# A two-layer hybrid transformer block on one core: three convolution taps per attention step, attention tiles in a list of their own, norm chunks ahead of context adds, modulation bias per four pairs

## The chip, the core and the metric

The kernel runs on one core of a Trainium2 chip. The metric is the time of one execution in microseconds (us) on the device. A core has five engines that each work through a queue of instructions in order and wait for each other by semaphores: TensorE (PE; PEld is its weight load), VectorE (DVE), ScalarE (ACT), GpSimd (POOL) and SyncE (SP), whose queue here issues the DMAs. TensorE writes into PSUM; everything else lies in SBUF.

## The reference, cut to what matters

Two layers act on 512 latent tokens and 256 context tokens of width 1024, all in fp32. The context goes through the same weights with another modulation, and in layer 1 only its keys and values are needed.

```
mod = silu(c) @ w_mod + b_mod            # shift, scale, gate, twice
xn = rms_norm(x) * (1 + scale1) + shift1
p = xn @ w_in                            # q, k, v | Fourier | conv | pool columns
attn = softmax(rope(norm(q)) @ rope(norm(k)).T) @ v      # 4 query heads, 2 key heads
four = real(fft2(p_f)) @ w_f
conv = silu(layer_norm(depthwise31(a * sigmoid(b)) + bias)) @ w_pw
pool = (window means - u) @ w_pool * scale
x = x + gate1 * (concat(attn, four, conv, pool) @ w_out)
xn = rms_norm(x) * (1 + scale2) + shift2
x = x + gate2 * ((silu(xn @ w_a) * (xn @ w_g)) @ w_ffn_out)   # inner width 2816
```

## The kernel before

Activations lie transposed: a tile has 128 channels on the partitions and tokens along the free axis (512 latent, then 256 context). Every fp32 product is made of three fp32r matmuls (`mm3`, line 315) on operands split into a rounded part and a remainder, so each weight is loaded raw by a DMA, rounded by ScalarE and subtracted by GpSimd or VectorE (`split`, line 180).

SBUF is handed out in lists of buffers. `W` (line 77) has 14 buffers of 1024 columns: raw weights, their two parts, modulation weights, and the transposed probabilities `pt` of attention. `AL` (line 74) has 28 buffers of 768 columns: normalized inputs, mixer outputs, Fourier pieces, and the query tiles `qst` and `qT`. A tile takes a buffer when it is first written, in the order in which the program asks, and gives it back after its last reader. PSUM has two buffers each of three kinds; the kind `PB` (two banks) holds the scores `S`, the running sum `run` of the convolution and the gate products. Within these rules a scheduler orders each engine's queue by a simulated time line, with the order of the program as priority; it looks at what is ready, so an instruction can run well ahead of its place.

Each layer has a mixer (`mix_phase`, line 599) and a feed-forward part (`ffn`, line 1204).

In the mixer, the projection to q, k and v comes first. Then the loop of line 1110 runs over attention tiles (one block of 128 queries and one head; 24 in layer 0, of which the last 8 are context queries with only 256 keys, 16 in layer 1) plus two steps. Step i computes the scores of tile i and their softmax (`soft`: maximum on VectorE, line 995; exp and scale on ScalarE), takes one pair of modulation columns from `mod_pairs` (two 512 KB weight loads, 16 small matmuls, a transpose, a sum, a bias add in line 344), lets `fill` take other projection work (columns for convolution, pooling and Fourier, then the Fourier mixer, then the convolution's layer norm) by declared costs in us at `pace.fill` per step, transposes and multiplies with v the tile of step i - 2 (`flip`), and pulls convolution taps:

```
pull(pace.taps0)
for i in range(len(tiles) + 2):
    ...
    if i >= pace.step0:
        pull(pace.taps)
        for _ in range(pace.side): next(side, None)
pull(99)
```

A tap is one VectorE instruction over all tokens of a block of 128 channels (line 669). The convolution has 31 taps and two blocks; of block 1 the first `side_n` taps (10 in layer 0, 8 in layer 1) run on ScalarE and GpSimd. `taps0`, `step0` and `taps` are 6, 3, 2 in layer 0 and 10, 2, 2 in layer 1. `tail` (line 1078) begins the layer norm after the convolution (`conv_out`) only when the generator of taps is exhausted; until then it gives Fourier work, and then nothing. What is left is written after the loop, behind the taps that are left and the casts of the attention outputs (`mix_at`). The output projection follows: 8 output blocks, of which the last four are held for the second half of the tokens.

In the feed-forward part of layer 0 a chunk of 128 inner channels is done by a seven-product scheme (`fast`, line 1251): `load_ff` (line 229) loads the two weight columns of a chunk raw, and makes seven operands of them, each in one `W` buffer. The first two chunks are done directly (`fast_first`, line 1227). After every two chunks `out_step` (line 1355) multiplies with the output weights and adds to x, latents first, then context; in the last step it also squares x for the next norm, whose reciprocal root is made by `n1.rstd`. The normalized chunks (`apply`, line 454) are written in the next layer's mixer. Layer 1's feed-forward part uses plain products (`ag`, line 1343).

## Time and profile before

| | us |
|---|---|
| median of 3 runs | 1476.47 (1474.7 to 1476.76) |
| the profiled execution | 1474.25 |
| its span, first to last instruction | 1472.5 |
| TensorE busy | 1417.3 (96%) |
| VectorE busy | 945.2 (64%) |
| ScalarE busy | 600.2 (41%) |
| GpSimd busy | 199.3 (14%) |

Busy time is what the engine's instructions cover. TensorE's matmuls overlap in the records and their ends are modelled, so a stretch that is all busy need not be at its peak. PEclk is the clock that TensorE was granted, 1.00 being 2.4 GHz and 0.50 being 1.2 GHz. The stages in the profiled execution, roughly: start and first projection to 76 us, the rest of layer 0's mixer to 336 us, its feed-forward part to 874 us, layer 1's mixer to 1102 us, its feed-forward part to the end.

### The profile page before, as it was taken

How to read it: one execution, taken by the hardware profiler on the slowest of the kernel's cores; microseconds unless marked ns; L12 is line 12 of the kernel's file. 1: busy time of each engine (PE TensorE's matmuls, PEld its weight loads, DVE VectorE, ACT ScalarE, POOL GpSimd, SP SyncE). 2: the span in 40 equal slices, each digit the busy share in tenths (PEclk: the TensorE clock that was granted, in tenths of full speed). 3: DMA queues.
4: the chain of work that ended last, by engine and by line, in shares of the span. 5: the costliest groups of instructions: out<-in, count | busy, mean ns of one | idle time of the engine just before them, and what ended most of it. 6: DMA issues, size and time to landing. Idle time of an engine off the chain costs nothing.

```text
span 1472.5 us, 20702 instructions
## 1 busy us (share of the span) xinstructions
PE 1417.3 (96%) x8298; PEld 1217.2 (83%) x8298; DVE 945.2 (64%) x1572; ACT 600.2 (41%) x1035; POOL 199.3 (14%) x161
## 2 busy tenths in 40 slices
PE   7999988999999999999999989999899999999998
PEld 4787766998998999999999968776698888888887
DVE  3569577247986778686877777866545545444444
ACT  4457656436533233332332345666544322222220
POOL 2526420420000000000000035430240000000000
PEclk9999989999999999999999999999999999999999
DMA  9525433320323133222322233356442323333231
GB/s 297 164 87 165 157 110 107 109 71 26 104 70 103 54 91 114 87 68 76 115 86 58 92 111 92 117 169 211 127 114 80 108 86 90 111 101 100 89 98 57
DMA packets 192928, 157.35 MB, mean 107 GB/s; under 512 B 6464, under 2 KB 179520, under 8 KB 192832
## 3 DMA queue, kind: packets, MB, share of 16 engines
q1 hardware_dynamic: 192544, 155.34, 34.4%
q8 instruction: 65, 1.06, 0.3%
q10 hardware_dynamic: 288, 0.69, 0.1%
q14 instruction: 31, 0.25, 0.1%
HBM read 151.81 MB, written 4.19 MB: 106 GB/s over the span
## 4 chain that ended last, share of the span: by engine, by line
PE 83%; DVE 7%; ACT 4%; DMA 4%; issue 1%; POOL 1%; SPq 0%; ACTq 0%; DVEq 0%; POOLq 0%
PE ag L161 35%; PE fo L161 20%; PE wo L161 6%; PE qkv L161 4%; PE cv L161 3%; PE agl L161 3%; PE mod L161 3%; DVE run L669 3%; PE u L161 2%; PE ssq L161 1%; PE S L161 1%; DMA wm<-in_w_mod_dram 1%; PE pv L161 1%; PE PT L167 1%; PE cc L161 1%
## 5 line engine op out<-in xcount | busy, mean ns | idle before, releaser
L1362 DVE SCALAR_TENSOR_TENSOR x<-fo,mod,x 128x512 f32<-128x512 f32 (+1 forms) x264 | 170.7, 657 | 81.0 <-PE fo L161 80.5
L161 PE MATMUL fo<-hl,foh 128*128 128x512 f32 (+1 forms) x528 | 187.7, 356 | 0.0
L161 PE MATMUL fo<-hh,fol 128*128 128x512 f32 (+1 forms) x528 | 187.4, 356 | 0.0
L161 PE MATMUL fo<-hh,foh 128*128 128x512 f32 (+1 forms) x528 | 185.5, 358 | 1.9 <-DVE x L1362 1.4
L161 PE MATMUL ag<-t,fs 128*128 128x384 f32 x720 | 136.6, 336 | 0.9 <-DVE hg L1266 0.9
L161 PEld LDWEIGHTS ag<-t,fs 128*128 128x128 f32 x720 | 125.0, 188 | 6.4 <-issue 1.6
L161 PEld LDWEIGHTS fo<-hh,foh 128*128 128x128 f32 x528 | 99.0, 188 | 16.1 <-DVE x L1362 1.8
L161 PEld LDWEIGHTS fo<-hh,fol 128*128 128x128 f32 x528 | 99.2, 188 | 15.1 <-issue 0.2
L161 PEld LDWEIGHTS fo<-hl,foh 128*128 128x128 f32 x528 | 99.2, 188 | 14.7 <-issue 0.7
L182 ACT CAST foh<-fo 128x1024 fp32r<-128x1024 f32 x44 | 46.2, 1050 | 146.0 <-DMA fo<-in_w_ffn_out_dram 146.0
L161 PE MATMUL ag<-b,fa 128*128 128x384 f32 x480 | 92.6, 336 | 1.5 <-DVE ht L1216 1.5
L105 DVE TENSOR_TENSOR fol<-fo,foh 128x1024 fp32r<-128x1024 f32 x44 | 53.8, 1222 | 54.1 <-ACT foh L182 41.9
L669 DVE SCALAR_TENSOR_TENSOR run<-glu,vt,run 128x512 f32<-128x512 f32 (+1 forms) x98 | 87.0, 887 | 1.0
L161 PEld LDWEIGHTS ag<-b,fa 128*128 128x128 f32 x480 | 83.4, 188 | 3.4 <-DVE ht L1216 1.8
L242 ACT CAST fs<-ff 128x512 fp32r<-128x512 f32 x80 | 45.4, 620 | 75.0 <-DVE ff L246 53.0
L437 POOL TENSOR_TENSOR acca<-acca,sq 128x512 f32<-128x512 f32 (+1 forms) x4 | 4.5, 1117 | 523.8 <-ACT sq L436 523.8
L161 PE MATMUL wo<-mxh,wol 128*128 128x384 f32 (+2 forms) x224 | 73.7, 330 | 0.0
L161 PE MATMUL wo<-mxl,woh 128*128 128x384 f32 (+2 forms) x224 | 73.5, 329 | 0.0
L161 PE MATMUL wo<-mxh,woh 128*128 128x384 f32 (+2 forms) x224 | 73.5, 331 | 0.1
L161 PE MATMUL ag<-xfh,fah 128*128 128x512 f32 (+1 forms) x192 | 71.3, 376 | 1.2 <-ACT xfh L465 1.2
L161 PE MATMUL ag<-xfl,fah 128*128 128x512 f32 (+1 forms) x192 | 71.6, 373 | 0.8 <-DVE xfl L466 0.8
L242 ACT CAST fa<-ff 128x512 fp32r<-128x512 f32 x60 | 35.6, 619 | 90.2 <-PE ag L161 51.7
(319 smaller groups left out, 3308.1 us busy)
## 6 DMA issues: line engine op xcount, KB each, us to landing
wm<-in_w_mod_dram SPq DMA_DIRECT2D x64, 512.0 KB, 4.4
fo<-in_w_ffn_out_dram SPq DMA_DIRECT2D x44, 512.0 KB, 3.3
ff<-in_w_ffn_in_dram SPq DMA_DIRECT2D x40, 512.0 KB, 4.7
fa<-in_w_ffn_in_dram SPq DMA_DIRECT2D x24, 512.0 KB, 4.4
fg<-in_w_ffn_in_dram SPq DMA_DIRECT2D x24, 512.0 KB, 3.9
wm<-in_w_mod_dram SPq DMA_DIRECT2D x40, 256.0 KB, 5.3
wo<-in_w_out_dram SPq DMA_DIRECT2D x16, 512.0 KB, 4.8
wm<-in_w_mod_dram SPq DMA_DIRECT2D x16, 384.0 KB, 3.3
```

The lines of the kernel that those rows point to most:

```text
L105: eng.tensor_tensor(out=out, in0=full, in1=b32(hi), op=ALU.subtract)
L161: i = last_pe[0] = pe.matmul(*a, **kw)
L167: i = last_pe[0] = pe.transpose(*a)
L182: act.copy(out=hi[:, :n], in_=raw[:, :n])
L242: act.copy(out=hi, in_=full)
L437: eng.tensor_tensor(out=a, in0=a, in1=t[:, sl], op=ALU.add)
L669: yield dve.scalar_tensor_tensor(out=cacc[b][:, :cwid] if j == CONVW - 1 else run, in0=glu[b][:, j:j + cwid], scalar=tap(b, j), in1=cacc[b ...
L1362: dve.scalar_tensor_tensor(out=x[m][:, sl], in0=ps[:, :n], scalar=modT[l][:, 40 + m, st:st + 1], in1=x[m][:, sl], op0=ALU.mult, op1=ALU.add)
```

## The change

Convolution taps per step become three in both layers. A new list `AT` of four buffers of 768 columns takes `qst`, `qT`, `pt` (one buffer per attention tile, no longer shared by a pair) and the raw weights of `load_ff`; `W` falls from 14 buffers to 11, which is the same room. `load_ff` loads a chunk's raw weights as four halves of 256 KB. The modulation bias is added, and the norm gain scaled, once per four pairs. In `fast_first` the second part of the tokens does the two products of one chunk over all eight input blocks, and then those of the other. In the last step of layer 0's feed-forward part, the rest of the modulation pairs is finished and the first two chunks of layer 1's normalized latents are written between the latents' and the context's `out_step`.

```diff
@@ -44,7 +44,7 @@
 FAST = (True, False)
-PACE = (Pace(12, 6, 3, 2, 4, 3.0, 0.7, 10), Pace(8, 10, 2, 2, 2, 3.0, 0.3, 8))
+PACE = (Pace(12, 6, 3, 3, 4, 3.0, 0.7, 10), Pace(8, 10, 2, 3, 2, 3.0, 0.3, 8))
@@ -57,7 +57,8 @@
     alp = ctx.enter_context(tc.tile_pool(name="alp", bufs=28))
-    wp = ctx.enter_context(tc.tile_pool(name="wp", bufs=14))
+    wp = ctx.enter_context(tc.tile_pool(name="wp", bufs=11))
+    tp = ctx.enter_context(tc.tile_pool(name="tp", bufs=4))
     dp = ctx.enter_context(tc.tile_pool(name="dp", bufs=1, space=bass.MemoryType.DRAM))
@@ -76,6 +77,9 @@
         return wp.tile([P, 1024], dt, tag="w", name=name)
+
+    def AT(name, dt=F32):
+        return tp.tile([P, T], dt, tag="at", name=name)
@@ -229,11 +233,11 @@
         raws = []
-        for o in (0, DFF):
-            raw = RAW("ff")
-            nc.sync.dma_start(out=raw.rearrange("p (a b) -> p a b", b=P), in_=rows(w_ffn_in[l][:, o + P * c:o + P * c + P]))
+        for o, i in ((0, 0), (0, 1), (DFF, 1), (DFF, 0)):
+            raw = AT("ff")[:, 0:512]
+            nc.sync.dma_start(out=raw.rearrange("p (a b) -> p a b", b=P), in_=rows(w_ffn_in[l][512 * i:512 * i + 512, o + P * c:o + P * c + P]))
             raws.append(raw)
-        a1, a2, g1, g2 = (r[:, 512 * i:512 * i + 512] for r in raws for i in range(2))
+        a1, a2, g2, g1 = raws
         ops = {}
@@ -339,11 +343,13 @@
                 tr(ps[:, 128 * c:128 * c + 128], me[:, 128 * c:128 * c + 128], ident)
-            m2 = modT[l][:, 2 * q:2 * q + 2, :]
-            dve.tensor_reduce(out=m2, in_=ps[:, 0:256].rearrange("p (c g w) -> p c w g", c=2, g=4)[:, :, 0:2, :], axis=AX.X, op=ALU.add)
-            dve.tensor_tensor(out=m2, in0=m2, in1=vcol(l, V_BM + 2 * q, 2).unsqueeze(2).to_broadcast([P, 2, 2]), op=ALU.add)
-            if q // 4 in (1, 4):
-                scaled_gain(l, q // 12, 2 * q % 8, 2 * q % 8 + 2)
+            dve.tensor_reduce(out=modT[l][:, 2 * q:2 * q + 2, :], in_=ps[:, 0:256].rearrange("p (c g w) -> p c w g", c=2, g=4)[:, :, 0:2, :],
+                              axis=AX.X, op=ALU.add)
+            if q % 4 == 3:
+                v = modT[l][:, 2 * q - 6:2 * q + 2, :]
+                dve.tensor_tensor(out=v, in0=v, in1=vcol(l, V_BM + 2 * q - 6, KD).unsqueeze(2).to_broadcast([P, KD, 2]), op=ALU.add)
+                if q // 4 in (1, 4):
+                    scaled_gain(l, q // 12, 0, KD)
         raws = fetch_w(q0)
@@ -962,7 +968,7 @@
             j, o = qpos(i)
-            st = AL("qst")
+            st = AT("qst", F32R)
             src = qsb[j][:, o:o + 256].rearrange("p (h d) -> p h d", h=4)
@@ -970,7 +976,7 @@
                 tr(ps[:, P * h:P * h + P], b32(st[:, P * h:P * h + P]), ident)
-            qTs[i] = AL("qT")
+            qTs[i] = AT("qT", F32R)
             act.copy(out=qTs[i][:, 0:512], in_=ps[:, 0:512])
@@ -998,26 +1004,25 @@
-            def flip(self, pt_):
-
-                e = self.h % 2
+            def flip(self, pair):
+
+                self.pt = AT("pt")
                 for j, (c0, n) in enumerate(((0, 2),) if self.nk == 2 else ((0, 4), (4, 2))):
...
                         tr(pt[:, P * c:P * c + P], self.pr[:, P * (c0 + c):P * (c0 + c) + P], ident)
-                    dst = pt_[j][:, 512 * e:512 * e + P * n]
+                    dst = self.pt[:, P * c0:P * (c0 + n)]
                     if j:
...
                         act.copy(out=dst, in_=pt[:, 0:P * n])
-                if not e:
+                if self.h % 2 == 0:
                     return
...
                     for g in range(2):
-                        o = 512 * g + P * (c % 4)
-                        mm(po[64 * g:64 * g + 64, 0:P], v, pt_[c // 4][:, o:o + P], start=c == 0, stop=c == self.nk - 1,
+                        mm(po[64 * g:64 * g + 64, 0:P], v, pair[g].pt[:, P * c:P * c + P], start=c == 0, stop=c == self.nk - 1,
                            tile_position=(0, 64 * g))
@@ -1106,17 +1111,13 @@
         pull(pace.taps0)
-        pt_ = None
         for i in range(len(tiles) + 2):
...
             if i >= 2:
-                t = tiles[i - 2]
-                if t.h % 2 == 0:
-                    pt_ = [W("pt", F32) for _ in range(1 if t.nk == 2 else 2)]
-                t.flip(pt_)
+                tiles[i - 2].flip(tiles[i - 3:i - 1])
             fill(pace.fill * (1 - pace.share))
@@ -1236,14 +1237,12 @@
                     A.second(norm, l, second)
-                for k in range(KD):
-                    if z:
-                        nm = ("b12", "b22")[k // 4]
-                    else:
-                        nm = ("b11", "b21")[k // 4]
-                    xh, xl = A.h(nm, k % 4), A.l(nm, k % 4)
-                    for i in range(4):
-                        mm3(out[i], ws[i][0][:, P * k:P * k + P], ws[i][1][:, P * k:P * k + P], xh, xl, k == 0, k == KD - 1)
+                for pair in ((0, 1), (2, 3)) if z else ((0, 1, 2, 3),):
+                    for k in range(KD):
+                        nm = f"b{1 + k // 4}{1 + z}"
+                        for i in pair:
+                            mm3(out[i], ws[i][0][:, P * k:P * k + P], ws[i][1][:, P * k:P * k + P], A.h(nm, k % 4), A.l(nm, k % 4),
+                                k == 0, k == KD - 1)
                 for c in range(2):
@@ -1287,6 +1286,7 @@
         def fast_steps():
+            nxt = None
             fast_first()
@@ -1303,12 +1303,19 @@
                             n1.rstd(sl)
+                            if st == 0:
+                                for _ in filler:
+                                    pass
+                                nxt = Acts("xn")
+                                for k in range(2):
+                                    n1.apply(l + 1, 0, k, sl, st, nxt)
                 else:
...
                 next(filler, None)
+            return nxt
@@ -1370,8 +1377,9 @@
         ns = NF // 2
+        nxt = None
         if FAST[l]:
-            fast_steps()
+            nxt = fast_steps()
         else:
@@ -1403,7 +1411,7 @@
             pass
-        return n1
+        return n1, nxt
@@ -1428,7 +1436,7 @@
         filler = mod_pairs(1, 0, 8, False) if l == 0 else iter(())
-        norm, A = ffn(l, *nxt, filler), None
+        norm, A = ffn(l, *nxt, filler)
...
 def _constants():
```

## Rows read from the trace of the kernel before

**Rows 1.** The page, part 1: busy us, share of the span, instructions.

```profile
PE 1417.3 (96%) x8298; PEld 1217.2 (83%) x8298; DVE 945.2 (64%) x1572; ACT 600.2 (41%) x1035; POOL 199.3 (14%) x161
```

**Rows 2.** Busy time in stretches of the span.

```profile
core 0: us, PE busy (x) PEld busy (x) DVE busy (x) ACT busy (x) POOL busy (x), PEclk, DMA share, GB/s
104.00:160.00 56.00, 52.61 (x437) 41.27 (x436) 49.81 (x69) 40.79 (x68) 33.14 (x22) 1.00 0.43 138
160.00:190.00 30.00, 29.50 (x278) 24.81 (x280) 9.86 (x26) 14.31 (x30) 6.90 (x9) 1.00 0.55 176
190.00:262.00 72.00, 58.94 (x432) 44.59 (x427) 56.52 (x117) 46.83 (x107) 6.54 (x6) 0.86 0.32 96
420.00:820.00 400.00, 399.15 (x2348) 372.04 (x2348) 305.54 (x537) 129.65 (x230) 0.00 (x0) 1.00 0.29 87
850.00:882.00 32.00, 26.63 (x148) 21.97 (x147) 24.33 (x32) 13.12 (x22) 12.00 (x15) 0.95 0.35 115
1003.00:1047.00 44.00, 42.51 (x401) 30.28 (x400) 35.31 (x83) 29.31 (x57) 4.71 (x2) 1.00 0.76 232
1047.00:1070.00 23.00, 18.89 (x78) 14.53 (x76) 4.81 (x15) 10.11 (x15) 5.27 (x3) 0.85 0.25 72
```

**Rows 3.** VectorE's time line, layer 0: start, us, line, operation, idle before.

```profile
174.21 1.82 DVE L995 TENSOR_REDUCE st<-S 128x1 f32<-128x768 f32 x2 [0.29 <-PE S L161]
...
205.31 1.02 DVE L669 SCALAR_TENSOR_TENSOR run<-glu,vt,ca 128x783 f32<-128x783 f32 x1
...
235.56 1.03 DVE L669 SCALAR_TENSOR_TENSOR ca<-glu,vt,run 128x783 f32<-128x783 f32 x1
...
239.13 0.42 DVE L995 TENSOR_REDUCE st<-S 128x1 f32<-128x256 f32 x1 [0.80 <-PE S L161]
```

**Rows 4.** VectorE's groups by form, 104 to 262 us: busy, mean ns, idle before.

```profile
L669 DVE SCALAR_TENSOR_TENSOR run<-glu,vt,run 128x783 f32<-128x783 f32 x48 | 49.5, 1031 | 0.4
...
L344 DVE TENSOR_TENSOR mod<-mod,vt 128x4 f32<-128x4 f32 x16 | 8.6, 536 | 0.2
```

**Rows 5.** TensorE's time line, layer 0, first matmul of the output projection.

```profile
262.32 0.45 PE L161 MATMUL wo<-mxh,woh 128*128 128x384 f32 x1
```

**Rows 6.** ScalarE's time line, layer 0, a table load.

```profile
253.82 1.28 ACT L997 ACT_TABLE_LOAD   x1
255.11 0.47 ACT L997 ACTIVATE pr<-S,st 128x256 f32<-128x256 f32 x1
```

**Rows 7.** VectorE's time line, layer 1.

```profile
1003.46 0.96 DVE L995 TENSOR_REDUCE st<-S 128x1 f32<-128x768 f32 x1 [1.09 <-PE S L161]
...
1019.49 0.75 DVE L669 SCALAR_TENSOR_TENSOR run<-glu,vt,ca 128x512 f32<-128x512 f32 x1
...
1045.95 0.75 DVE L669 SCALAR_TENSOR_TENSOR ca<-glu,vt,run 128x512 f32<-128x512 f32 x1
```

**Rows 8.** Chain of waits, layer 1: start, us, what.

```profile
1070.20 18.89 PE wo L161 x133
```

**Rows 9.** TensorE's time line at the layer boundary.

```profile
878.46 1.12 PE L161 MATMUL ssq<-acca,ones 128*128 128x256 f32 x2 [3.98 <-POOL acca L437]
...
882.11 0.48 PE L161 MATMUL qkv<-wqh,xnh 128*128 128x512 f32 x1
```

**Rows 10.** What TensorE waited for, 341 to 420 us: us, times, longest.

```profile
PE ag L161 <- DVE ht L1216: 1.5, 1, 1.5
```

**Rows 11.** The page, part 6: DMA issues, KB, us to landing.

```profile
ff<-in_w_ffn_in_dram SPq DMA_DIRECT2D x40, 512.0 KB, 4.7
```

**Rows 12.** Chain of waits: one product of layer 0, layer 1's gate load.

```profile
420.50 2.08 PE ag L161 x12
...
1093.71 5.31 DMA fg<-in_w_ffn_in_dram
...
1099.09 1.06 ACT fgh L182
...
1100.18 1.23 DVE fgl L105
```

## The prediction, made before the run

> **What bounds the kernel now.** I read the page first: TensorE is busy 1417.3 of 1472.5 us [rows 1], so only some 55 us of idle time, and whatever the clock takes, can be won. Then the busy time by stage [rows 2], to see where those 55 us lie. The feed-forward stage of layer 0 (420 to 820 us) leaves 0.85 us of 400 idle: nothing to win there, something to lose. The end of layer 0's attention (190 to 262 us) is the poor place: 13.1 us idle, and a granted clock of 0.86. With 1.00 at 2.4 GHz and 0.50 at 1.2 GHz, 0.86 is 28% of the stage at the lower level: 20 us in which work takes twice as long, so up to 10 us more. The layer boundary (850 to 882) has 5.4 us idle; the end of layer 1's attention (1003 to 1070) 1.5 + 4.1 us, with a clock of 0.85 in its last 23 us (30%, 6.9 us at the low level, up to 3.4 us lost). Then VectorE's view of the first of these: it is busy 49.8 of 56 us from 104 to 160 us, 9.9 of 30 from 160 to 190, 56.5 of 72 from 190 to 262. So VectorE is full, idle, full again, and behind its second full stretch TensorE waits. The reader is to see that order, not the 64% mean.
>
> **Taps, layer 0.** The loop over 26 steps (24 attention tiles) pulls 6 taps ahead and then some per step from step 3. Block 0 has 31 taps, block 1 has 21. With two per step, block 1's first tap is the 32nd pull, 6 + 2(i - 2) >= 32, step 15; with three, 6 + 3(i - 2) >= 32, step 11. The program's order counts because the accumulator of block 1 takes one of two PSUM buffers that the scores use too, handed out in that order. The trace bears it out: VectorE was two thirds idle from 160 to 190 us, and yet block 1's first tap comes at 205.31, its last at 235.56 [rows 3]. The maxima of tiles 10 and 11 are at 174.2 [rows 3], so taps can start at about 177. VectorE is free 20.1 of 30 us from 160 to 190 [rows 2], so some 0.67 x 17 = 11 us of the 17 between there and 194 (an estimate). At 1.03 us a tap [rows 4] that is 11 of the 21 taps, and VectorE's second full stretch ends 11 us earlier, 235.6 to about 224.
> What is late next: the eight narrow tiles, which start at 239.13 [rows 3] after the last tap, then the convolution's layer norm (transposes, a square root, silu, two matmul groups). Two things move them. The query tiles leave the 28-buffer list, in which inputs, mixer outputs and Fourier pieces live, for a list of four, so they need not wait for Fourier buffers. And the generator is exhausted at step 18 (the 53rd pull), so the norm is written before the last tiles instead of after the loop. I count Fourier as written by step 17 (38 of declared cost before it at 3.0 a step, then 10.4). The output projection begins at 262.32 [rows 5].
> Value: 13 us, the 11 that VectorE gives back and 2 for narrow tiles that no longer wait. Upper end 23: all idle time and all low clock of the stage [rows 2]. Lower end -3: from step 11 on, not 15, the scores of four tiles have one PSUM buffer instead of two, some 0.8 us each for a maximum (0.95 [rows 3]) that no longer overlaps.
> ScalarE pays for the mixing of exp, square root and silu: a table load took 1.28 us and the exp behind it began at once, 253.82 + 1.28 = 255.10 against 255.11 [rows 6]. I take four more loads, 5 us on an engine with 25 of 72 us free, hidden, and inside the lower end.
> The Trainium skill, "ScalarE: Activation LUTs" (What ACT_TABLE_LOAD costs), adds a drain of about 1.38 us to each switch; by that the four cost 10.6 us, still inside ScalarE's free time but close to the serial end of the stage. The row shows no such drain, and I go by the row.
>
> **Taps, layer 1.** 18 steps, 10 taps ahead, 31 + 23 in all. Block 1 starts at 10 + 2(i - 1) >= 32, step 12, and 12 taps are left for after the loop; with three, step 9, and all are done at step 16. Tile 9's maximum is at 1003.46, block 1's first tap at 1019.49, its last at 1045.95 [rows 7]. VectorE is free 8.7 of 44 us there [rows 2]; from 1019.49 on 23 taps of 0.75 us and the tiles between them fill it, so the free time lies ahead of them, 8 us of taps move into it, and the last comes at about 1038. Behind it the norm's chain runs to 1070.20, where the projection resumes [rows 8]; TensorE is idle 4.1 us in it and 6.9 us slow. With the norm written before the mixer's casts its transposes no longer stand behind projection matmuls. Value 6; upper end 9 (1.5 + 4.1 + 3.4 [rows 2]); lower end -3, the DMA being at 0.76 of its time there [rows 2], with modulation weights that pace the tiles whatever VectorE does.
>
> **Norm chunks ahead of context adds.** TensorE waits 3.98 us for the context sums and starts layer 1's projection at 882.11 [rows 9]. The first two chunks' normalized latents don't need those sums; with them ready by 874.5, where the wait begins (878.46 - 3.98), 24 matmuls are there for the hole. They cost VectorE four instructions in front of the context adds, and one pending modulation pair has to be finished first (two transposes, done by then). Value 4, the wait; upper end 5.4, the stage's idle time [rows 2]; lower end -2, adds late behind them.
>
> **Bias per four pairs.** 40 adds become 10. In layer 0's attention 16 took 8.6 us [rows 4], a mean of 536 ns for 128x4, so some waited. 12 go, three quarters: 6.4 us of VectorE, most of it before 160 us, where TensorE is idle 3.4 us [rows 2]. Value 1, ends 0 and 3.
> The Trainium skill, "SBUF — State Buffer" (Who interferes with whom), makes the port pair of VectorE and GpSimd an exclusive lock: the loser blocks for the whole instruction. By it the adds that waited beside GpSimd (33 of 56 us busy) give back their excess only if the next VectorE instruction does not block in their stead; taps read PSUM and would not.
>
> **First feed-forward products.** In the second half two products are finished before the other two, so the gating of the first pair starts 48 matmuls earlier. The wait for it was 1.5 us [rows 10]. Value 1; ends +1.5 and, since operands are then wanted twice as fast, -3.
>
> **The lists.** Four tiles of 768 take the place of three of 1024; the pair loads of layer 0 become four 256 KB halves instead of two of 512 KB (40 issues [rows 11] become 80; DMA share 0.29 in the stage [rows 2], so hidden). In attention the three buffers come back, since probabilities no longer use that list. Elsewhere they are gone. I count the places. (a) Both ends of the mixer: four output weights are held (8 buffers) while four gate weights (8) come. With 14 the fourth gate load waits for a release already: in layer 1 it is issued at 1093.71, after a projection, and is on the path: 5.31 to land, 1.06 and 1.23 to split [rows 12], 7.6 us. With 11, three loads wait instead of one; releases follow each other by one projection, so the last comes later by part of that, and TensorE has the first pair's products meanwhile. Layer 0's projections are wider and leave more time. I take 2 us there and 3 in layer 1, ends 0 and 7.6 each. (b) Layer 0's feed-forward: seven operands and two output weights (4) make 11, just enough; before, raws took two of the 14, so it is 12 against 11. One buffer less delays an operand by at most one product, which I take as nothing in most steps: 2 us; ends 0 and 20 (ten steps, a product of 12 matmuls taking 2.08 [rows 12]). (c) The start of the kernel: 0.5, ends 0 and 3.
>
> **Sum.** Gains 13 + 6 + 4 + 1 + 1 = 25; losses 2 + 3 + 2 + 0.5 = 7.5; net -17.5. The profiled execution took 1474.25 us (a span of 1472.5 and 1.75 around it): 1474.25 - 17.5 = 1456.8. The median of the runs, 1476.47, is 2.2 above it, so the time to forecast is 1459.
>
> **Rivals.**
> A, more comes back: the stage from 190 us closes up nearly whole (23), layer 1 gives 9, the boundary 5: gain 39, loss 4: 1476.5 - 35 = 1441. For it: three engines have free time in that stage. Against it: the chain max, exp, reciprocal, scale, transpose, copy is serial in every tile, and now has one score buffer for longer.
> B, the taps move and the end does not: scores with one PSUM buffer, the modulation DMA and ScalarE's table loads take VectorE's place as the last wait; only boundary, adds and a few us remain, less the losses: -3, 1473. For it: a DMA share of 0.76 in layer 1. Against it: in layer 0's stage VectorE is the fullest engine after TensorE, 56.5 of 72 us, and the DMA share is 0.32 [rows 2].
> C, slower: the weight list of 11 binds in the feed-forward stages. Price: both mixer ends at 7.6 and 20 us in layer 0's stage, 35 in all, against gains of 25: 1486. It decides from about 1.2 us a pair, over the 20 pairs of layer 0, where gains and losses cancel. For it: loads there already wait for releases, and the stage has no idle time to hide in. Against it: operands are cut well ahead, and TensorE takes output products in between.
>
> **Chances.** Forecast (1448 to 1468) 0.55, A 0.17, B 0.14, C 0.14. A measurement of this kernel tells 0.2%, 3 us, from no change. Faster by more: the forecast, A, half of B: 0.79; within: half of B and a little of C: 0.08; slower: 0.13. The range 1438 to 1477 leaves out the far end of A (0.06) and C.
>
> **What would show it.** Right: block 1's first tap after tile 11 in layer 0 and tile 9 in layer 1; VectorE busier from 175 to 194 us and its last tap near 224; the first projection matmul near 250; clock 1.00 from 200 on; no 4 us hole at the boundary, the first qkv products before the context sums. Wrong: narrow tiles still last, with ScalarE ahead of them; new waits for gate weights before the first feed-forward matmul; idle time over 2 us in layer 0's feed-forward. Any idle time there above 20 us makes the whole prediction wrong.

## The result: 0.6% slower, and where the time went

The changed kernel takes 1484.82 us (1483.57 to 1485.74, median of 4 runs) against 1475.59 us: a ratio of 1.0059, 95% interval [1.0047, 1.0072]. Slower by some 9 us, where 1459 was forecast, outside the range of 1438 to 1477. The profiled execution took 1483.57 us with a span of 1481.8. TensorE is busy 1426.1 us of it, 8.8 more than before with the same 8298 matmuls.

Busy time of the changed kernel in the stretches of [rows 2] (columns as there):

```profile
104.00:160.00 56.00, 53.88 (x451) 42.51 (x449) 48.40 (x66) 42.87 (x70) 32.55 (x22) 1.00 0.44 138
160.00:190.00 30.00, 30.00 (x289) 25.27 (x288) 20.66 (x33) 14.13 (x30) 6.68 (x8) 1.00 0.62 195
190.00:262.00 72.00, 62.36 (x467) 48.54 (x465) 41.41 (x97) 47.18 (x106) 14.30 (x10) 0.96 0.49 144
420.00:820.00 400.00, 400.00 (x2375) 376.04 (x2373) 304.80 (x531) 129.82 (x231) 0.00 (x0) 1.00 0.27 84
850.00:882.00 32.00, 25.52 (x139) 21.19 (x138) 23.54 (x34) 12.03 (x22) 9.21 (x13) 0.88 0.24 66
1003.00:1047.00 44.00, 39.49 (x359) 26.74 (x362) 28.11 (x63) 21.63 (x45) 0.00 (x0) 0.94 0.76 237
1047.00:1070.00 23.00, 18.96 (x77) 12.32 (x69) 9.15 (x20) 12.81 (x20) 8.54 (x4) 0.75 0.28 75
```

Layer 0's stages are better than before: VectorE's hole from 160 to 190 us is half filled, the next stretch has more work done at a higher clock, and the feed-forward stage has no idle time at all. Of these stretches the loss is in the last three; what lies between 882 and 1003 us they do not cover. To follow it, I mark three points in each time line: the last matmul of layer 0's output projection, of layer 0's feed-forward output, and of layer 1's output projection. Times in us. The median is that of each kernel's runs, and the ratio beside it is to the kernel before on the same chip; the last four columns come from the one profiled execution of each.

| kernel | median | ratio, 95% | layer 0 mixer ends | its feed-forward takes | layer 1 mixer takes | of it, to the last key transpose |
|---|---|---|---|---|---|---|
| before | 1475.59 | | 336.1 | 538.4 | 226.3 | 61.3 |
| changed | 1484.82 | 1.0059 [1.0047, 1.0072] | 332.2 | 536.8 | 242.0 | 67.4 |
| lists_alone | 1478.29 | 1.0015 [1.0003, 1.0026] | 334.6 | 531.5 | 238.5 | 72.7 |
| taps_alone | 1485.18 | 1.0055 [1.0037, 1.0073] | 344.8 | 538.8 | 232.8 | 61.2 |
| chunks_alone | 1478.19 | 1.0016 [1.0005, 1.0026] | 336.7 | 544.1 | 224.3 | 58.9 |
| bias_pairs | 1481.39 | 1.0030 [1.0020, 1.0040] | 333.2 | 538.9 | 235.4 | 68.0 |
| old_lists | 1480.94 | 1.0028 [1.0018, 1.0038] | 340.3 | 543.6 | 222.4 | 58.1 |
| taps2_l1 | 1481.86 | 1.0035 [1.0021, 1.0049] | 332.4 | 537.5 | 236.6 | 71.0 |
| taps2_both | 1487.25 | 1.0075 [1.0061, 1.0089] | 337.2 | 536.9 | 234.8 | 70.0 |
| early_mod | 1488.96 | 1.0086 [1.0071, 1.0102] | 332.5 | 556.4 | 225.0 | 69.5 |
| early_mod_taps2_l1 | 1491.47 | 1.0100 [1.0082, 1.0118] | 333.2 | 556.1 | 228.4 | 69.8 |
| x_pool | 1483.40 | 1.0056 [1.0043, 1.0069] | 333.6 | 537.1 | 240.4 | 70.9 |
| ahead0 | 1481.18 | 1.0045 [1.0033, 1.0057] | 332.9 | 537.4 | 238.3 | 68.2 |
| wm_al | 1490.25 | 1.0111 [1.0096, 1.0126] | 333.8 | 537.6 | 245.8 | 69.2 |
| q_and_al | 1485.58 | 1.0073 [1.0055, 1.0092] | 331.6 | 531.5 | 247.0 | 77.4 |
| z14 | 1481.99 | 1.0036 [1.0024, 1.0048] | 334.0 | 538.2 | 236.2 | 67.1 |
| z14_all | 1476.60 | 1.0001 [0.9992, 1.0010] | 334.3 | 543.5 | 226.4 | 61.5 |
| w12_at3 | 1463.11 | 0.9908 [0.9895, 0.9922] | 328.9 | 531.7 | 229.4 | 68.2 |
| after_12_3 | 1468.05 | 0.9948 [0.9936, 0.9961] | 330.9 | 537.7 | 227.0 | 58.2 |
| w12_pairbias | 1459.71 | 0.9897 [0.9881, 0.9912] | 330.7 | 531.4 | 223.0 | 63.8 |

The change wins 3.9 us in layer 0's mixer and 1.6 in its feed-forward part, which also took over 24 of layer 1's projection matmuls (5.7 us in chunks_alone), and loses 15.7 in layer 1's mixer; layer 1's feed-forward is 1 us shorter.

How the 15.7 us divide shows in TensorE's busy time and clock over that whole mixer: the kernel before, the changed kernel, and after_12_3, which is the changed kernel with one weight tile more (columns as in [rows 2]).

```profile
874.48:1100.75 226.27, 208.38 (x1461) 167.70 (x1462) 148.61 (x275) 128.88 (x227) 86.47 (x56) 0.98 0.45 136
869.04:1111.03 241.99, 217.59 (x1435) 169.50 (x1436) 142.34 (x254) 126.96 (x224) 79.79 (x50) 0.92 0.42 127
868.59:1095.60 227.01, 207.66 (x1435) 165.18 (x1436) 146.40 (x253) 126.22 (x223) 85.76 (x54) 0.96 0.44 135
```

Idle time grows by 6.5 us, from 17.9 to 24.4. The other 9.2 us are busy time, with 26 fewer matmuls: the granted clock is 0.92 for 0.98. By these means some 39 us of the stage ran at 1.2 GHz, for 9 before (estimates from the clock column and the lengths). So the loss shows twice, as idle time and as a lower clock, and the second is the larger part. Both come back together: with the same 1435 matmuls after_12_3 has 5.0 us less idle time and 9.9 less busy time than the changed kernel.

Layer 1 falls behind at its very start, with the last projection weight. SyncE asks for it only when GpSimd has split an earlier one (3.6 us of waiting, at 867.14), ScalarE waits for it, and the squares of the context stand behind its cast:

```profile
871.08 1.04 ACT L186 CAST wqh<-wq 128x1024 fp32r<-128x1024 f32 x1 [4.93 <-DMA wq<-in_w_in_dram]
```

```profile
869.00:879.00 10.00, 4.82 (x15) 3.00 (x15) 5.21 (x6) 4.06 (x8) 4.72 (x3) 0.76 0.32 102
```

In after_12_3 that load goes out at 861.23, and TensorE's wait for the squares (2.4 us) is not there. The same goes on in the load of layer 1's convolution weights (eight DMAs into four buffers), in the kernel before:

```profile
871.57 21.82 SPq L199 DMA_DIRECT2D wc<-in_w_in_dram  x8
```

and in the changed kernel, with what SyncE waited for ahead of it from 860 to 912 us (us in total, times, longest), ScalarE's cast of one of them, TensorE's wait from 905 to 925 us, and its busy time:

```profile
868.95 30.79 SPq L203 DMA_DIRECT2D wc<-in_w_in_dram  x8
```

```profile
SPq L203 <- POOL wcl L109: 17.1, 3, 7.8
...
SPq L203 <- DMA wc<-in_w_in_dram: 9.8, 3, 3.9
```

```profile
904.13 1.05 ACT L186 CAST wch<-wc 128x1024 fp32r<-128x1024 f32 x1 [7.81 <-DMA wc<-in_w_in_dram]
```

```profile
PE cv L165 <- ACT glu L767: 3.3, 1, 3.3
```

```profile
910.00:920.00 10.00, 6.67 (x29) 5.20 (x29) 5.71 (x10) 5.57 (x8) 2.37 (x1) 1.00 0.46 141
```

The reader is to see a chain with no overlap: a raw weight is asked for only when the one before has landed and GpSimd has split it, because with 11 buffers there is one to load into. ScalarE stands 7.81 us in front of the cast; the copies of q and k out of PSUM and the convolution's gate stand behind it, and for the gate TensorE is idle 3.3 of 10 us. Before, it was busy 10.00 there.

The end of the same mixer is late for a second reason. TensorE's last modulation pairs come behind their weights, one by one; the chain of waits (start, us, what) and the windows in which they lie:

```profile
1026.88 0.57 PE mod L165 x8
1027.51 9.39 DMA wm<-in_w_mod_dram
1037.56 9.09 DMA wm<-in_w_mod_dram
1046.79 1.08 PE mod L165 x8
1047.87 0.62 PE mods L171 x2
1048.49 1.06 PE mod L165 x8
```

```profile
1030.00:1040.00 10.00, 7.77 (x72) 4.12 (x68) 1.55 (x6) 1.66 (x5) 0.00 (x0) 1.00 1.09 351
1040.00:1050.00 10.00, 7.51 (x54) 2.04 (x54) 0.52 (x3) 1.12 (x4) 0.00 (x0) 0.57 1.02 299
1050.00:1060.00 10.00, 8.10 (x30) 5.65 (x30) 5.80 (x15) 7.11 (x10) 7.03 (x3) 0.75 0.20 57
```

The DMA engines are full, TensorE idles a quarter of 20 us, and then the granted clock falls to 0.57, most of the stretch at 1.2 GHz: eight matmuls of a pair take 1.08 us there, and 0.57 ahead of it. One load of 9.24 us stands in this chain in the kernel before, too; here there are two.

### The profile page after: what moved, and what is told of

Same layout as the page of the kernel before. It is cut to its first block, busy times and chain, and to the rows that moved or that the text cites. A ratio compares the mean times of both kernels' runs of the same rounds, so it can differ in the third digit from the quotient of the medians.

```text
span 1481.8 us, 20788 instructions
## 1 busy us (share of the span) xinstructions
PE 1426.1 (96%) x8298; PEld 1220.8 (82%) x8298; DVE 938.2 (63%) x1533; ACT 597.7 (40%) x1034; POOL 194.6 (13%) x161
## 5 line engine op out<-in xcount | busy, mean ns | idle before, releaser
L165 PE MATMUL ag<-xfh,fal 128*128 128x512 f32 (+1 forms) x192 | 71.5, 372 | 0.0
L165 PE MATMUL ag<-xfh,fgh 128*128 128x512 f32 (+1 forms) x192 | 71.3, 372 | 0.0
```

The lines of the kernel that those rows point to most:

```text
L165: i = last_pe[0] = pe.matmul(*a, **kw)
```

## Experiments

Each is named as in the table; the edits are shown abbreviated. The first theory (L) was that the list of 11 starves layer 1's modulation weights; the rival (T), that three taps per step do it.

**old_lists**, the changed kernel with the lists as before:

```
-wp bufs=11, tp bufs=4        # pt, qst, qT, ff in AT
+wp bufs=14                   # pt, ff in W; qst, qT in AL
```

> The changed kernel with the lists of the kernel before: 14 weight tiles, attention tiles back in the two old lists, layer 0's pair loads as two halves of 512 KB. Taps, norm chunks, bias and pair order stay changed. Theory L (the list of 11 holds back layer 1's modulation weights, and the mixer's end with them): the last modulation matmul of layer 1 ends near 1035 us instead of 1049, the projection's end moves up by the 10 us that were lost there, and the gains ahead of it stay; 1466 us, between 1460 and 1472. Rival T (three taps per step in layer 1 put the lateness there): the last modulation matmul stays near 1049 and the time within 3 us of the changed kernel, 1482 to 1488. Rival S (SyncE's queue, held by the loads of x, delays the modulation weights whatever the list is): as T, with the same wait rows.

Measured 1480.94, between the two ranges. Layer 1's mixer is well again, 222.4 us, as L has it, but layer 0 lost as much: its mixer ends 8.1 us later and its feed-forward is 6.8 longer than with the new lists. Neither theory had seen that the lists *win* time in layer 0.

**lists_alone**, the kernel before with `wp bufs=11`, `tp bufs=4` and the tiles in them:

> The kernel before with the lists of the changed kernel and nothing else. Theory L: layer 1's modulation matmuls end some 11 us later than before (1038 becomes about 1049) and the whole is 8 to 14 us slower, 1484 to 1490 us. Rival T: within 3 us of the kernel before, 1473 to 1479.

Measured 1478.29, in T's range. The last modulation matmul is late (1048.96), as L has it, but the mixer's 12.2 us are 11.4 us old at the last key transpose, before attention begins: ScalarE's cast and TensorE's idle time behind it, in this kernel:

```profile
899.79 1.05 ACT L186 CAST wch<-wc 128x1024 fp32r<-128x1024 f32 x1 [7.00 <-DMA wc<-in_w_in_dram]
```

```profile
910.00:920.00 10.00, 2.82 (x13) 2.00 (x11) 3.07 (x8) 4.58 (x10) 3.15 (x2) 0.74 0.20 58
```

**taps_alone**, `taps` 3, 3 in the kernel before:

```
-PACE = (Pace(12, 6, 3, 2, ...), Pace(8, 10, 2, 2, ...))
+PACE = (Pace(12, 6, 3, 3, ...), Pace(8, 10, 2, 3, ...))
```

> The kernel before with three taps per step in both layers and nothing else. Theory L: layer 0's scores end earlier, and the time is the same or better, 1466 to 1476 us. Rival T: layer 1's modulation matmuls end 8 to 12 us later and the time is 1480 to 1488.

Measured 1485.18, so T in the total. The profiled execution was the slowest of six (1488.82, 14.6 above the profiled one of the kernel before); of these 8.7 us are in layer 0's mixer, which no theory had named, and 6.5 in layer 1's. ScalarE's time line shows why. The query tiles of the last eight narrow attention tiles still come from the list of 28:

```profile
230.91 0.43 ACT L968 CAST qst<-q 128x256 fp32r<-128x256 f32 x1
...
258.15 0.41 ACT L968 CAST qst<-q 128x256 fp32r<-128x256 f32 x1
...
261.39 1.28 ACT L997 ACT_TABLE_LOAD   x1
```

The second of them stands behind the whole layer norm of the convolution, which three taps put ahead of it, and the scores of the last four tiles run on to 269 us, where the kernel before had ended its scores at 251.

**taps2_l1** and **taps2_both**, the changed kernel with `taps` 3, 2 and with 2, 2:

> The changed kernel with two taps per step in layer 1, three in layer 0. Theory L: the late modulation weights stay, 1480 to 1488 us, and the last modulation matmul of layer 1 within 3 us of 1049. Rival T: 1470 to 1476, with the last modulation matmul near 1038.

> The changed kernel with two taps per step in both layers. Theory L2: with the new lists the third tap in layer 0 gives 0 to 3 us, so this is no faster than the kernel with two in layer 1 alone: 1481 to 1486. Rival P (the third tap takes PSUM from the scores in layer 0 whatever the lists are, as in the kernel with three taps alone, where layer 0's mixer ended 8.7 us later): 1472 to 1477.

Measured 1481.86 and 1487.25. L's range and its late matmul (1048.58) hold in the first; the second lies above both ranges. With the query tiles in their own list the third tap wins 4.8 us in layer 0 (337.2 against 332.4); in layer 1 it costs 5.4 of the mixer and 3.0 in the medians. So L and T each have a part of it.

**chunks_alone**, the norm chunks of the diff in the kernel before:

> The kernel before with the norm chunks ahead of the context adds and nothing else. As predicted for the changed kernel: the hole of 4 us at the layer boundary closes, 1470 to 1474. Rival H (the head norm and rope chain of ScalarE and VectorE behind the projection takes the gain back): layer 1's keys are transposed no earlier than before, 1475 to 1478.

Measured 1478.19, slower by some 2 us. Rival H has it: the last key transpose ends at 939.6, for 935.8 before. Busy time at the boundary, and VectorE behind the context sums:

```profile
874.00:880.00 6.00, 6.00 (x35) 5.16 (x33) 4.65 (x7) 3.19 (x6) 3.58 (x7) 1.00 0.40 126
880.00:886.00 6.00, 4.78 (x23) 3.29 (x22) 1.37 (x3) 2.66 (x6) 3.88 (x7) 1.00 0.47 138
886.00:892.00 6.00, 3.91 (x17) 3.09 (x18) 5.90 (x10) 3.59 (x6) 1.89 (x1) 0.85 0.15 41
```

```profile
885.84 1.75 DVE L451 RECIPROCAL R<-R 128x256 f32<-128x256 f32 x1 [4.08 <-ACT R L450]
```

The hole is not closed, it is moved: 24 matmuls run in it, and 3.3 us of idle time follow, because VectorE makes the other normalized chunks behind the context's reciprocal root, and stands 4.08 us for that.

**early_mod** and **early_mod_taps2_l1** move eight of layer 1's pairs into layer 0's feed-forward (with one more `next(filler)` a step; the second also has `taps` 3, 2):

```
-mod_pairs(l, 8, 24) ... mod_pairs(1, 0, 8, False)
+mod_pairs(l, 16 if l else 8, 24) ... mod_pairs(1, 0, 16, False)
```

> The changed kernel, but eight of layer 1's sixteen modulation pairs are computed in layer 0's feed-forward steps, where their weights stand in the tiles of the softmax list, so that eight fewer pairs want buffers of the list of 11 in layer 1's attention. Theory L2 (in layer 1's mixer the list of 11 costs 12 us and more, by late modulation weights; the third tap costs 5 to 7 there): the last modulation matmul of layer 1 comes before 1040 us; layer 0's feed-forward grows by 12 us (8 pairs of 1.07 + 0.44 us), layer 1's mixer shrinks by 20 to 25: 1472 to 1478. Rival V (what is late in layer 1 is VectorE's chain of tiles and taps, and the modulation weights only lie beside it): the mixer shrinks by the moved matmuls alone, 10 to 12, and the time stays within 3 us of the changed kernel, 1482 to 1488.

> As the kernel with eight modulation pairs moved, and two taps per step in layer 1 instead of three. Theory L2: both costs of layer 1 are gone, 1466 to 1473, faster than the kernel before. Rival V: the taps alone count, 1478 to 1483.

Measured 1488.96 and 1491.47, above every range. In the first, layer 1's mixer shrinks by 17.0 us, 5 more than the moved work of 12, so the late weights seem to cost something; layer 0's feed-forward grows by 19.6, 2.45 a pair. The first part speaks for late weights, the price kills it.

**x_pool** (reloads of x issued by GpSimd), **ahead0** (no early output weight in the Fourier part) and **wm_al** (layer 1's modulation weights in the list of 28) each take away one thing that held the modulation loads:

```
-nc.sync.dma_start(out=x[k][:, LAT], in_=lat[k])     # x_pool, layer 1
+pool.dma_start(out=x[k][:, LAT], in_=lat[k])
-ahead[0] = 1                                        # ahead0
+ahead[0] = 0 if last else 1
-raw = W("wm", F32)                                  # wm_al, layer 1
+raw = AL("wm", F32)                                 # three of 768
```

> The changed kernel with layer 1's eight reloads of x issued by GpSimd instead of SyncE. In the changed kernel's trace SyncE issues four of them between 1005.72 and 1019.85 us, each waiting for the attention to release its tile, with 14 modulation loads behind them in the same queue. Theory Q (these waits in SyncE's queue hold the modulation loads): layer 1's last modulation matmul ends 6 to 12 us earlier than 1049, the time is 1473 to 1480. Theory L2 (the list of 11 has no free tile for them anyway until the Fourier part ends): the last modulation matmul ends at 1046 or later, 1482 to 1488.

> The changed kernel without the early load of layer 1's first output weight during the Fourier part: two to three of the 11 tiles stay free for modulation weights there. Theory L2: one more pair is in flight from 993 us on, the last modulation matmul ends 4 to 8 us earlier, 1477 to 1482. Theory Q: the reloads of x still stand ahead of 14 modulation loads, nothing moves, 1483 to 1488.

> The changed kernel with layer 1's modulation weights in the list of 28 (three tiles of 768 a pair) instead of the list of 11. Theory L2: with no modulation weight in the list of 11, the last modulation matmul ends 8 us earlier or more, 1472 to 1479. Theory Q: SyncE's order still has four reloads of x ahead of seven pairs, the gain is under 4 us, 1481 to 1487.

Measured 1483.40, 1481.18 and 1490.25; the last modulation matmul ends at 1051.07, 1049.83 and 1058.88. Theory Q falls, and so does L2 as it stood: with no modulation weight in the list of 11 they come later still. (ahead0's time is in L2's range, but its last modulation matmul is no earlier.) In all three the last key transpose is 68 to 71 us behind the feed-forward, as in the changed kernel: what they mend lies after the place where the time is lost. **q_and_al**, two of them with `taps` 3, 2 and no chunks, ends no better:

> The changed kernel with two taps per step in layer 1 (three in layer 0), no norm chunks ahead of the context adds, the reloads of x on GpSimd and layer 1's modulation weights in the list of 28. If L2 or Q, or both, hold: layer 0 as in the kernel with the lists alone or 2 to 3 us better (864 to 868 us to its end, where the kernel before has 874.5), layer 1's mixer within 3 us of the kernel before: 1462 to 1470. If neither holds: 1478 to 1484, layer 1's mixer 8 us or more above the kernel before.

Measured 1485.58, above both ranges, with layer 1's mixer 20.7 us longer than before.

**z14** and **z14_all**: one list of 14 as before, only layer 0's query tiles moved into it; z14 with `taps` 3, 2, no chunks, bias and pair order as changed, z14_all with all other edits of the change.

```
-st = AT("qst", F32R)
+st = AL("qst") if last else W("qst")[:, 0:T]        # qT likewise
```

> One list of 14 weight tiles again, no list apart: probabilities and pair loads as in the kernel before, and only layer 0's query tiles move, from the list of 28 into the list of 14. Three taps per step in layer 0, two in layer 1, bias per four and pair order as changed, no norm chunks. Theory W (the length of the weight list is what layer 1 lost by; the query tiles' release from the list of 28 is what layer 0 gained by): layer 0's mixer ends near 332 us as in the changed kernel, layer 1 runs from the feed-forward's end to the projection's end in 224 to 229 us as before: 1468 to 1474. Rival N (layer 1's loss comes from the order of its loads in the queue, not from the length): 232 us or more there, 1478 to 1484.

> The same single list of 14, with layer 0's query tiles in it, and all else as in the changed kernel: three taps in both layers, norm chunks too. Against the kernel with the old lists (1480.94 us) only layer 0's query tiles differ. Theory W: layer 0's mixer ends near 332 us instead of 340.3, the rest stays: 1470 to 1475. If the third tap takes PSUM from the scores in layer 0 whatever the query tiles do: 338 us or later, 1478 to 1483.

Measured 1481.99 and 1476.60. z14_all does what theory W says in layer 1 (226.4) and, against old_lists, in layer 0 (334.3 for 340.3), though the time lies 1.6 us above W's range. z14 misses in layer 1 (236.2), the figure that the rival N had. In z14 layer 1's first projection matmul comes 12.7 us behind the feed-forward, for 7.6 before; the next kernel shows this other cause by itself.

**bias_pairs**, the kernel before with the bias per four pairs and the pair order:

> The kernel before with the bias per four pairs and the pair order of the first feed-forward products, nothing else. As predicted: 1 us each, 1473 to 1476. If either costs what they were meant to give: 1477 to 1480.

Measured 1481.39, layer 1's mixer at 235.4 as in z14. VectorE's time line at its boundary:

```profile
874.60 0.55 DVE L439 TENSOR_TENSOR acda<-acda,sq 128x256 f32<-128x256 f32 x1
879.60 0.17 DVE L342 TENSOR_REDUCE mod<-mods 128x4 f32<-128x16 f32 x1 [4.45 <-PE mods L167]
879.81 0.18 DVE L346 TENSOR_TENSOR mod<-mod,vt 128x16 f32<-128x16 f32 x1
...
881.57 1.67 DVE L324 SCALAR_TENSOR_TENSOR a<-mod,vt 128x16 f32<-128x16 f32 x1
883.34 0.75 DVE L465 SCALAR_TENSOR_TENSOR xt<-x,a,R 128x512 f32<-128x512 f32 x1
```

The eighth of layer 1's early pairs is finished behind the context sums. With one bias for four pairs the gains of all eight chunks now hang on it, so VectorE stands 4.45 us and the first normalized chunk is made at 883.34, 11 us behind the last feed-forward matmul. The norm chunks hide this where both edits are in, because they draw the last pair forward.

**w12_at3**: 12 weight tiles and 3 attention tiles, one of the two pair loads back in the weight list, `taps` 3, 2, no chunks. **after_12_3**: the same lists in the changed kernel, nothing else.

```
-wp bufs=11, tp bufs=4; raw = AT("ff")[:, 0:512]     # four halves
+wp bufs=12, tp bufs=3; gg = RAW("ff")               # two halves in W, two in AT
```

> 12 weight tiles and 3 attention tiles instead of 11 and 4; one of the two pair loads in layer 0's feed-forward stands in the weight list again. Three taps in layer 0, two in layer 1, no norm chunks. Theory W: layer 1's stage from the feed-forward's end to the projection's end, 242.0 us in the changed kernel and 226.3 before, comes to 230 to 236: 1472 to 1479. Rival N: 238 or more, 1480 to 1486.

> The changed kernel with 12 weight tiles and 3 attention tiles instead of 11 and 4 (one of layer 0's two pair loads stands in the weight list), nothing else. Theory W: the list of 11 is what made the change slower: layer 1 from the feed-forward's end to the projection's end comes from 242.0 us to 230 to 235, layer 0's mixer to about 329: 1468 to 1475, faster than the kernel before. If the third tap in layer 1 and the norm chunks, which the kernel w12_at3 leaves out, are the larger part: 1478 to 1484.

Measured 1463.11 and 1468.05: theory W holds, and both do better in layer 1 than it forecast (229.4 and 227.0). The changed kernel with one weight tile more is 16.8 us faster in the medians, and faster than the kernel before. Layer 1's mixer comes from 242.0 to 227.0 us, 9.2 of these 15.0 before the last key transpose. The pair loads that changed with the lists stand in layer 0's feed-forward, which is no shorter (537.7 for 536.8). Layer 1's convolution weights, and what SyncE now waits for ahead of them from 860 to 912 us:

```profile
868.27 19.50 SPq L203 DMA_DIRECT2D wc<-in_w_in_dram  x8
```

```profile
SPq L203 <- PE qkv L165: 12.9, 2, 7.9
...
SPq L203 <- PE fo L165: 6.9, 1, 6.9
```

This load's waits for GpSimd's split and for the load before are gone; what is left, but for 1.8 us, are releases by TensorE's own progress.

**w12_pairbias**, w12_at3 with the bias after every pair:

> The kernel w12_at3 (1463.11 us) with the bias added after every modulation pair, as in the kernel before. Theory B (with one bias for four pairs the gains and shifts of all of layer 1's norm wait for the last of the eight pairs, which is finished behind the context sums): the first projection matmul of layer 1 comes 7 to 8 us behind the last feed-forward matmul instead of 12.8, and the time falls by 4 to 6 us: 1457 to 1460. If the bias costs nothing at the boundary: 1462 to 1466, the adds coming back.

Measured 1459.71, the lowest median of all and 1.0% below the kernel before. Theory B holds for the place: in its VectorE time line the first normalized chunk follows the last context square at once, at 865.28, and the first projection matmul comes 7.0 us behind the feed-forward, for 12.8. The mixer is 6.4 us shorter. In the total the gain is not clear of noise: 3.4 us between medians from two chips, 1.8 when each is set against the kernel before on its chip, with intervals that overlap.

```profile
864.80 0.55 DVE L442 TENSOR_TENSOR acda<-acda,sq 128x256 f32<-128x256 f32 x1
865.28 1.21 DVE L468 SCALAR_TENSOR_TENSOR xt<-x,a,R 128x512 f32<-128x512 f32 x1
```

## Why the prediction was wrong, point by point

**Taps, layer 0: the mechanism right, the term mis-sized (+13 forecast, some 5 measured).** What was to show it in VectorE's order is there, and more of it; the clock is not, 0.96 from 190 to 262 us where 1.00 was forecast. Block 1's first tap and its last, against 205.31 and 235.56 in [rows 3]; the same for layer 1, against 1019.49 and 1045.95 in [rows 7]:

```profile
171.61 1.02 DVE L675 SCALAR_TENSOR_TENSOR run<-glu,vt,ca 128x783 f32<-128x783 f32 x1
...
211.28 1.03 DVE L675 SCALAR_TENSOR_TENSOR ca<-glu,vt,run 128x783 f32<-128x783 f32 x1
...
998.07 0.74 DVE L675 SCALAR_TENSOR_TENSOR run<-glu,vt,ca 128x512 f32<-128x512 f32 x1
...
1029.93 0.75 DVE L675 SCALAR_TENSOR_TENSOR ca<-glu,vt,run 128x512 f32<-128x512 f32 x1
```

The first projection matmul comes at 235.66, for 262.32 in [rows 5]. And the projection ends only 3.9 us earlier. What is late next was named (the norm) but not priced: ScalarE, in order, waits for output weights ahead of the norm's copies, and the serial chain behind them has lost its cover. ScalarE and TensorE there:

```profile
242.07 1.04 ACT L186 CAST woh<-wo 128x1024 fp32r<-128x1024 f32 x1 [4.35 <-DMA wo<-in_w_out_dram]
...
248.36 1.04 ACT L186 CAST woh<-wo 128x1024 fp32r<-128x1024 f32 x1 [2.92 <-DMA wo<-in_w_out_dram]
...
255.80 1.28 ACT L1049 ACT_TABLE_LOAD   x1
257.10 0.30 ACT L1049 ACTIVATE mv<-mv,epst 128x6 f32<-128x6 f32 x1
```

```profile
258.22 3.62 PE L171 MATMUL lnB<-ident,zt 128*128 128x128 f32 x12 [3.42 <-DVE zt L1053]
```

The second half of the step, that the query tiles leave the list of 28, was counted at 2 us. By taps_alone it is the condition of the whole gain: without it the third tap costs 8.7 in the profiled execution.

The table loads behave as forecast: 255.80 + 1.28 = 257.08, and the square root begins at 257.10. The drain of about 1.38 us that the Trainium skill, "ScalarE: Activation LUTs" (What ACT_TABLE_LOAD costs), adds shows neither here nor in [rows 6].

**Taps, layer 1: the sign was wrong (+6 forecast, -5.4 of the mixer measured).** The taps ended 16 us earlier (10.6 counted from the feed-forward's end), more than the 8 forecast, but the table load of the norm's square root came only 4.2 earlier (1055.08 for 1059.24), which is 1.3 later from that end, and behind modulation pairs that ended at 1049.5 for 1038.1. The prediction had their pace as its lower end, -3. The sign hangs on the rest of the kernel: with half the pairs moved out, the mixer is 3.4 us shorter with three taps than with two (early_mod and early_mod_taps2_l1, one profiled execution each). Whether the third tap still costs there with 12 weight tiles was not measured by itself.

**Norm chunks (+4 forecast, -2.0 measured alone).** The failed step is that the wait goes once there is work for the hole; the sums that ended the wait also feed the context's reciprocal root, behind which VectorE makes the other chunks. **Bias per four pairs (+1 forecast, -4.9 measured with the pair order in bias_pairs; -1.8 to -3.4 by w12_pairbias, not clear of noise).** The prediction counted the adds that go and not the readers that now wait for the fourth pair. That the exclusive port lock in the Trainium skill, "SBUF — State Buffer" (Who interferes with whom), returned anything here, no run shows: the cost is a wait for TensorE. **Pair order (+1)** was not run by itself; the wait of [rows 10] is gone in the changed kernel, but it is there in bias_pairs, whose feed-forward is no shorter.

**The lists: the step that failed.** Forecast were losses of 5 at the mixers' ends, 2 in layer 0's feed-forward and 0.5 at the start. The feed-forward *gained* 6.8 us (531.5 against 538.4, seen in lists_alone, q_and_al and both kernels of 12 tiles without chunks; kernels with the old pair loads stay at 538 or more), and the loss lies at a place that the count did not have, the start of layer 1's mixer: one weight tile more gives back 16.8 us, 15.0 of them in that mixer. There feed-forward output weights, projection weights and convolution weights meet in one list, and 11 leaves one raw tile in flight. "In attention the three buffers come back" was no help to the 9.2 us that are gone by then. The prediction had a price for the clock in its gains and none in its losses, and 9.9 of the 15.0 us are TensorE's busy time at a lower clock. Rival C had the total (1486) by luck: it put 20 us into the feed-forward stage. Even with 12 tiles the change gives 6.8 us (1468.05 for 1474.86 on that chip) and not 17.5; the rest is in the terms above.

**The edits interact.** Alone, lists, taps, chunks, and bias with pair order cost 2.0, 8.8, 2.0 and 4.9 us, 17.7 together; in one kernel 9.2. The lists pay the taps' cost in layer 0, and the chunks seem to hide part of the bias'. Adding terms one by one, as the prediction did, could not give the total.

**Open.** 12 and 3 differ from 11 and 4 in two lists and one pair load at once; that it is the weight tile rests on the waits that went and on the place, behind the last pair load. How the pair loads in halves shorten the feed-forward (2.6 us less idle time from 330 to 850 us, the rest some 0.4 us of busy time a step) was not taken apart.

## What to carry to other kernels

Here a list that was one buffer short cost where loads of two stages meet, not where most of its tiles are used: count raw tiles in flight at each stage boundary, and look for a load that waits for the split of the one before. When several small edits are batched, look for a shared condition (who must release what, who now waits for the last of a group), because one edit can be both the price and the cure of another. Price a wait of TensorE by the granted clock around it as well as by its length. And a stall is not won until the work behind it has been read for what it waits for next.

## What the runs showed of the hardware that was not expected

With the modulation loads of layer 1 left to the end, the DMA share reads 1.09 at 351 GB/s, and a 512 KB load in the chain took 9.39 us where the median of these loads from 925 to 1060 us is 5.1. The kernel before has a load of 9.24 us in its chain, at 1019.79. Moving eight DMAs from SyncE to GpSimd did not change the time by what can be measured (1483.40 against 1484.82). This agrees with the Trainium skill, "DMA: Bandwidth & Descriptors" (Rules for kernel authors), by which issuing from several engines saves only issue time.

The granted clock was 1.00 from 1030 to 1040 us, with TensorE busy 7.77 of 10 us with small matmuls, 0.57 in the next 10, with 7.51, and still 0.75 in the 10 behind, with 8.10. It also fell around the waits at the mixer's start (0.76 from 869 to 879 us) and stayed at 1.00 through the 3.3 us of idle time from 910 to 920. In q_and_al and wm_al, where these matmuls came later, the mixer was longer still.
